# The channel-major copy of the activations: turned by transposing DMAs in DRAM instead of by TensorE

## The chip, the cores and the metric

The kernel runs on one core of one Trainium2 chip. The metric is the device time of one launch in microseconds (us). Work is spread over TensorE (PE, with its weight loads listed as PEld), VectorE (DVE), ScalarE (ACT), GpSimd (POOL) and the DMA engines; nearly all DMAs are issued by SyncE (SP), in program order, into one queue.

## The reference

Four residual blocks are applied one after the other to a sequence of 2048 tokens with 1024 channels, all in float32. Each block has the same frame and its own mixers:

```python
h = x @ w_in                       # 1024 -> the channels of the mixers
mixed = concat(mixers(h))          # recurrences, attention, gated parts
z = x + mixed @ w_out              # 1024 -> 1024
x = layer_norm(z) * ln_g + ln_b    # blocks 1 to 3
```

Block 1 has a chunked recurrence (HGRN2) and sliding-window attention; block 2 a gated linear attention (GLA, chunks with a running state) and a spatial gating part whose input is normalised; block 3 a retention and a multi-scale pool; block 4, which normalises its input by its root mean square first, has a band attention, an mLSTM and a convolution. Within a block a token needs only itself and earlier tokens.

## The kernel before

The sequence is cut into four blocks of 512 tokens, and a **stage** is one layer of one block. Stages run in pairs of blocks: layer 1 of blocks 0 and 1, layer 2 of blocks 0 and 1, up to layer 4, and then the same for blocks 2 and 3. In what follows (2,0) is layer 2 of block 0. There are 16 stages, and 12 of them (layers 1 to 3) leave an activation that a later stage reads.

A stage reads its activation **by channel**: channels lie on partitions, tokens along the row. `load_x` fetches it in eight pieces of 128x512 into `u` tiles and splits each into a high part `ah` (a ScalarE cast to the rounded fp32r type) and a low part `al` (VectorE, the difference). Every product with weights is then three matmuls: high by high, high by low, low by high. Weights come in pieces. In the first pass over a layer a raw piece is loaded into `wst` (two buffers), split into `whl`, and stored in DRAM as `wdr`; later passes load `whl` from `wdr` ready split, 1 MB a piece, into four `whl` buffers. `next_w` hands out the next piece. The in-projection is a row of matmuls named `acc<-whl,ah`, `acc<-ah,whl` and the like; the mixers' small matmuls and transposes write to `mm` (PSUM). Then `out_proj` multiplies by `w_out`, adds the residual rows and normalises them in `big`, by token.

The normalised rows must be turned round for the next layer. That is `tail`, once for each 128 tokens: eight PE transposes (`mm<-ident,big`), ScalarE copies out of PSUM into two `t` tiles, two DMAs to the channel-major DRAM buffer `chn`, and a DMA of the rows themselves to `rows` (the next layer's residual). For tiles with an odd number the normalisation is already complete; for even ones the layer's scale and bias are applied by ScalarE in the copy (by channel), and VectorE applies them to the rows. The four tails of a stage wait in `self.pending`; `flush`, called at later groups of the in-projection, takes one out in the **next** stage. So (1,0) is turned during (1,1), and read by `load_x` of (2,0) after it.

Program order is not the final order. A list scheduler fixes, before the run, the static order of instructions on each engine; weights have a high priority. Each engine then works through its list in order and waits on semaphores. Scratch tiles come from rings: the tag `t` has 7 buffers of 2 KB a partition, handed out in program order to tails, to the mixers' exponentials and states and to much else, so a later `t` tile can't be written before the tile seven requests earlier has been read for the last time. The PSUM tag `mm` has four banks, `acc` four.

Of the kernel before, what the change touches and what calls it, by code (L numbers as in the profile page):

```python
# [10 lines left out]
F32 = mybir.dt.float32  # L11
F32R = mybir.dt.float32r
I32 = mybir.dt.int32
U8 = mybir.dt.uint8
BF16 = mybir.dt.bfloat16
AF = mybir.ActivationFunctionType
ALU = mybir.AluOpType
# [3 lines left out]
D = 1024  # L21
T = 2048
TB = 512
# [203 lines left out]
class Build:  # L227
# [114 lines left out]
    def setup(self):  # L342
        nc = self.nc
# [14 lines left out]
        nc.gpsimd.affine_select(out=cm, in_=ones[:, 0:128], compare_op=ALU.is_ge, fill=0.0, base=0, pattern=[[1, 128]], channel_multiplier=-1)  # L358
        self.cmask = self.const([128, 128], U8, "cmask")
        nc.vector.tensor_copy(self.cmask, cm)  # L360
# [3 lines left out]
        nc.gpsimd.affine_select(out=self.amask, in_=zero, compare_op=ALU.is_ge, fill=NEGB, base=0, pattern=[[1, 128]], channel_multiplier=-1)  # L364
        self.rst = self.const([128, 512], BF16, "rst")
        nc.vector.memset(self.rst, 1.0)
# [7 lines left out]
        self.pending, self.ahead, self.start = [], [], True  # L374
        self.kv, self.kv_at, self.turn = None, None, 0

        self.chn, self.rows = {}, {}
        for l in self.layers[:-1]:
            for i in range(2):
                self.chn[l, i] = self.dp.tile([4, 128, D], F32, tag=f"chn{l}{i}", name="chn")  # L380
                self.rows[l, i] = self.dp.tile([4, 128, D], F32, tag=f"rows{l}{i}", name="rows")

        lb = self.const([128, 4], F32, "lb")
# [15 lines left out]
        for n in ("hgw", "glag", "retg", "pscale", "mlg"):  # L399
            h = self.const([128, 4], F32, n + "h")  # L400
# [93 lines left out]
    def next_w(self, n=1024):  # L494
        if self.ahead:
            return self.ahead.pop(0)
        w = self.weight(self.wi, self.wpos, n)
        self.wpos += 1
        return w

    def group(self, ps, w, a, b):
# [54 lines left out]

    def load_x(self, b, l):
        if not self.start:
            for t in range(4):
                for i in range(2):  # L560
                    self.load_x1(b, l, t, i)
            return

        ws = []
        self.wi, self.wpos = "wi1", 0
        for parts in (((0, 0), (1, 0)), ((0, 1), (1, 1)), ((2, 0), (3, 0)), ((2, 1), (3, 1))):
            for t, i in parts:
                with self.hp():
                    self.load_x1(b, l, t, i)
            ws.append(self.next_w())  # L570
        self.ahead, self.start = ws, False
        self.lc = self.lconst(l, b)
        with self.later(300):
            self.save()
# [5 lines left out]
    def load_x1(self, b, l, t, i):  # L580
        nc = self.nc
        st = self.u()
        src = self.I["xt"][b] if l == 1 else self.chn[l - 1, b % 2]
        self.first(nc.sync.dma_start(st, src[t, :, i * 512:i * 512 + 512]))
        c = slice(t * 128, t * 128 + 128)
        h = self.ah[:, 4 * i:4 * i + 4, c]
        nc.scalar.copy(h, c4(st))  # L587
        self.tt(self.al[:, 4 * i:4 * i + 4, c], c4(st), h.bitcast(F32), ALU.subtract)

    def load_xr(self, b, l):  # L590
        self.xr = self.big(self.at, [128, 4, D], F32)
# [22 lines left out]
    def out_proj(self, layer, b, split):  # L614
        nc = self.nc
        wo = f"wo{layer}"
        alpha = {1: ALPHA1, 2: ALPHA2, 3: ALPHA2, 4: 1.0}[layer]
        last = layer == max(self.layers)
        if layer < 4:
            lng, lnb = [self.u() for _ in range(2)], [self.u() for _ in range(2)]  # L620
            for i in range(2):
                nc.sync.dma_start(lng[i], self.I["lnp"][2 * layer - 2:2 * layer - 1, i * 512:i * 512 + 512].partition_broadcast(128))
                nc.sync.dma_start(lnb[i], self.I["lnp"][2 * layer - 1:2 * layer, i * 512:i * 512 + 512].partition_broadcast(128))
        acc = [self.acc() for _ in range(4)]
        for j in range(4):
            hi, lo = self.weight(wo, j)
            hi = hi.rearrange("p (k c) -> p k c", k=2)
            lo = lo.rearrange("p (k c) -> p k c", k=2)
            if j == 0:
                split(0)  # L630
                split(1)
            for i in range(2):
                for t in range(4):
                    self.out_mm(acc[t], t, 2 * j + i, hi[:, i], lo[:, i])
                    if j < 3 and i == 1 and t == 1:
                        split(2 * j + 2)
                        split(2 * j + 3)
        sts = []
        for t in range(4):
            x = self.xr[:, t, 0:512]  # L640
            self.stt(x, x, alpha, acc[t], ALU.mult, ALU.add)
            if layer < 4:
                st = self.s(12, "bst")
                nc.vector.bn_stats(st[:, 0:6], x)
                sts.append(st)
        if self.todo:
            self.lc = self.lconst(*self.todo[0])
        ws = []
        acc = [self.acc() for _ in range(4)]
        for j in range(4):  # L650
            hi, lo = self.weight(wo, 4 + j)
            ws.append((hi.rearrange("p (k c) -> p k c", k=2), lo.rearrange("p (k c) -> p k c", k=2)))
        for t in range(4):

            if t % 2 == 0:
                for k in range(8):
                    hi, lo = ws[k // 2]
                    for t1 in (t, t + 1):
                        self.out_mm(acc[t1], t1, k, hi[:, k % 2], lo[:, k % 2])
            x = self.xr[:, t, 512:1024]  # L660
            self.stt(x, x, alpha, acc[t], ALU.mult, ALU.add)
            if layer == 4:
                nc.sync.dma_start(self.O[b * TB + t * 128:b * TB + t * 128 + 128, :], self.xr[:, t])
                continue
            st = sts[t]
            nc.vector.bn_stats(st[:, 6:12], x)
            x = self.xr[:, t]
            mv = self.s(2, "mv")
            nc.vector.bn_aggr(mv, st)
            y = self.rstd1(mv[:, 1:2], 1.0, 1e-5)  # L670
            if not last and t % 2 == 0:
                nm = self.s(1, "nm")
                self.stt(nm, mv[:, 0:1], -1.0, y, ALU.mult, ALU.mult)
                self.act(x, x, AF.Identity, scale=y, bias=nm)
                continue
            for i in range(2):
                xi = x[:, i * 512:i * 512 + 512]
                self.stt(xi, xi, mv[:, 0:1], lng[i], ALU.subtract, ALU.mult)
                self.stt(xi, xi, y, lnb[i], ALU.mult, ALU.add)
            if last:  # L680
                nc.sync.dma_start(self.O[b * TB + t * 128:b * TB + t * 128 + 128, :], x)
        if not last:
            xr = self.xr
            self.pending = [lambda t=t: self.tail(layer, b, xr, t, lng, lnb) for t in range(4)]
            if layer == 3:
                self.pending.append(lambda: self.rms_row(b, xr))

    def tail(self, layer, b, xr, t, lng, lnb):

        nc = self.nc  # L690
        x = xr[:, t]
        for j in range(2):
            ps = self.mm()
            for i in range(4):
                k = 4 * j + i
                self.tr(ps[:, i * 128:i * 128 + 128], x[:, k * 128:k * 128 + 128])
            f = self.t()
            if t % 2 and layer < 3:
                nc.scalar.copy(f, ps)
            else:  # L700
                for i in range(4):
                    o = slice(i * 128, i * 128 + 128)
                    if t % 2:
                        self.act(f[:, o], ps[:, o], AF.Copy, scale=self.col("ng", 4 * j + i))
                    else:
                        k = 8 * (layer - 1) + 4 * j + i
                        self.act(f[:, o], ps[:, o], AF.Identity, scale=self.lgn[:, k:k + 1], bias=self.lbn[:, k:k + 1])
            nc.sync.dma_start(self.chn[layer, b % 2][t, :, j * 512:j * 512 + 512], f)
        if t % 2 == 0:
            for i in range(2):  # L710
                xi = x[:, i * 512:i * 512 + 512]
                self.tt(xi, xi, lng[i], ALU.mult)
                self.tt(xi, xi, lnb[i], ALU.add)
        nc.sync.dma_start(self.rows[layer, b % 2][t], x)

    def rms_row(self, b, xr):

# [1095 lines left out]
def c4(ap):  # L1813
    return ap.rearrange("p (a b) -> p a b", a=4)
# [22 lines left out]
```

## Time and profile before

| | |
|---|---|
| time, median of 3 runs | 3685.87 us (3685.3 to 3686.74) |
| time of the profiled execution | 3691.55 us |
| its span | 3689.8 us |
| PE idle in the span (span less busy) | 37.7 us |
| DVE / ACT busy | 2256.2 us (61%) / 1389.5 us (38%) |
| DMA moved | 798.03 MB |
| mean granted TensorE clock | 0.999 |

The span is the time from the first to the last instruction that the profiler saw; the profiled execution's own time is 1.75 us longer. A row of the profile's groups gives an operation (out<-in by tile name, shape, count), its busy time and the mean of one; a row of the timeline gives start, duration and what it waited for. An engine's instructions overlap in the pipeline, so on PE the pace is read from start to start.

### The profile page before, as it was taken

The page shows a single profiled execution, that of the slowest core. Times are in us where ns is not written, and L with a number is a line of the kernel's source. Part 1 is how long each engine was busy: PE and PEld are TensorE (multiplying, and loading weights), DVE is VectorE, ACT ScalarE, POOL GpSimd, SP SyncE. Part 2 cuts the span into 40 slices and gives each one's busy share as a digit, 9 for nine tenths or more (in the row PEclk, how much of TensorE's full clock was granted, in tenths as well). Part 3 has the DMA queues.
Part 4 walks back from the last instruction along what each step waited for, and adds up shares of the span by engine and source line. Part 5 has one row for each costly group of instructions (what it writes and reads, how often), then busy time and mean ns, then how long its engine had stood idle before and what let it go on. Part 6 is the DMA issues. An engine that isn't in the chain of part 4 may idle for free.

```text
span 3689.8 us, 53341 instructions
## 1 busy us (share of the span) xinstructions
PE 3652.1 (99%) x20576; PEld 3090.4 (84%) x20576; DVE 2256.2 (61%) x5796; ACT 1389.5 (38%) x2890; POOL 14.9 (0%) x37
## 2 busy tenths in 40 slices
PE   8999999999999999999999999999999999999999
PEld 7888888888787888888888888989887878888887
DVE  7765566555755598587556556444454546883874
ACT  6636343323341355235254372313121313541451
POOL 0000000000000000000000000000000000000000
PEclk9999999999999999999999999999999999999999
DMA  7784577856885784853644645657475747446534
GB/s 274 252 291 156 199 266 278 296 182 231 308 305 202 249 288 166 296 189 104 215 180 167 251 167 185 241 178 267 161 259 182 275 176 254 149 145 208 184 114 160
DMA packets 161823, 798.03 MB, mean 216 GB/s; under 512 B 17952, under 2 KB 18080, under 8 KB 93984
## 3 DMA queue, kind: packets, MB, share of 16 engines
q1 hardware_dynamic: 161568, 794.62, 60.6%
q8 instruction: 162, 2.65, 0.3%
q14 instruction: 93, 0.76, 0.1%
HBM read 593.02 MB, written 201.52 MB: 215 GB/s over the span
## 4 chain that ended last, share of the span: by engine, by line
PE 60%; DVE 3%; ACT 1%; issue 0%; DMA 0%; SPq 0%; POOL 0%; POOLq 0%; DVEq 0%; ACTq 0%
PE acc L324 50%; PE mm L324 7%; PE mm L327 3%; DVE u L312 1%; DVE t L315 0%; DVE whl L315 0%; DVE big L312 0%; ACT t L302 0%; ACT u L301 0%; ACT t L301 0%; DMA wst<-in_wi_dram 0%; ACT whl L458 0%; DVE ss L1437 0%; ACT big L301 0%; DMA chn<-t 0%
## 5 line engine op out<-in xcount | busy, mean ns | idle before, releaser
L324 PE MATMUL acc<-whl,ah 128*128 128x512 f32 (+3 forms) x6144 | 1815.2, 379 | 2.8 <-DVE mix L312 1.9
L324 PEld LDWEIGHTS acc<-whl,ah 128*128 128x128 f32 x6144 | 1111.7, 188 | 226.2 <-issue 4.8
L324 PE MATMUL acc<-whl,al 128*128 128x512 f32 (+3 forms) x3072 | 1159.0, 377 | 0.0
L324 PE MATMUL acc<-ah,whl 128*128 128x256 f32 (+1 forms) x4096 | 1062.4, 343 | 9.1 <-ACT whl L458 8.3
L324 PEld LDWEIGHTS acc<-ah,whl 128*128 128x128 f32 x4096 | 699.4, 189 | 92.2 <-ACT whl L458 8.5
L324 PE MATMUL acc<-al,whl 128*128 128x512 f32 (+1 forms) x2048 | 697.1, 340 | 0.0
L324 PEld LDWEIGHTS acc<-whl,al 128*128 128x128 f32 x3072 | 578.2, 188 | 114.4
L324 PEld LDWEIGHTS acc<-al,whl 128*128 128x128 f32 x2048 | 386.7, 189 | 40.0 <-issue 3.6
L315 DVE TENSOR_TENSOR whl<-wst,whl 128x1024 fp32r<-128x1024 f32 (+3 forms) x141 | 167.0, 1185 | 112.2 <-ACT whl L458 109.6
L458 ACT CAST whl<-wst 128x1024 fp32r<-128x1024 f32 (+3 forms) x141 | 143.4, 1019 | 169.2 <-PE acc L324 102.2
L587 ACT CAST ah<-u 128x512 fp32r<-128x512 f32 x128 | 78.4, 620 | 271.5 <-PE acc L324 249.2
L312 DVE SCALAR_TENSOR_TENSOR big<-big,acc 128x512 f32<-128x512 f32 x128 | 86.3, 680 | 134.9 <-PE acc L324 134.6
L312 DVE SCALAR_TENSOR_TENSOR u<-mix,hdw,u 128x512 f32<-128x512 f32 x240 | 166.2, 741 | 0.3
L312 DVE SCALAR_TENSOR_TENSOR g<-g,acc 128x512 f32<-128x512 f32 x80 | 55.0, 687 | 162.3 <-ACT g L301 162.0
L301 ACT ACTIVATE g<-acc 128x512 f32<-128x512 f32 x72 | 42.9, 597 | 236.6 <-PE acc L324 236.5
L315 DVE TENSOR_TENSOR al<-u,ah 128x512 fp32r<-128x512 f32 x128 | 86.7, 680 | 51.5 <-ACT ah L587 51.4
L301 ACT ACTIVATE t<-mm,cols 128x128 f32<-128x128 f32 (+2 forms) x272 | 98.3, 462 | 51.2 <-PE mm L327 48.5
L324 PE MATMUL mm<-big,u 128*128 128x256 f32 (+2 forms) x616 | 92.4, 285 | 1.3 <-DVE u L315 1.3
L324 PEld LDWEIGHTS mm<-big,u 128*128 128x128 f32 x616 | 83.8, 189 | 6.7 <-DVE u L315 1.5
L1020 DVE CUSTOM_DVE_ANT_0 t<-mm,lc,nsk 128x256 f32<-128x256 f32 (+1 forms) x128 | 55.0, 472 | 49.4 <-PE mm L324 49.1
L324 PEld LDWEIGHTS mm<-vb,t 128*128 128x128 f32 (+1 forms) x640 | 67.9, 169 | 16.1 <-issue 9.5
L324 PE MATMUL mm<-vb,t 128*64 128x128 f32 (+2 forms) x640 | 78.8, 278 | 1.6 <-DVE t L312 0.9
(338 smaller groups left out, 4062.3 us busy)
## 6 DMA issues: line engine op xcount, KB each, us to landing
whl<-wdr SPq DMA_DIRECT2D x396, 1024.0 KB, 4.8
wdr<-whl SPq DMA_DIRECT2D x132, 1024.0 KB, 4.9
wst<-in_wi_dram SPq DMA_DIRECT2D x99, 512.0 KB, 6.2
rows<-big SPq DMA_DIRECT2D x48, 512.0 KB, 4.7
chn<-t SPq DMA_DIRECT2D x96, 256.0 KB, 3.5
u<-chn SPq DMA_DIRECT2D x96, 256.0 KB, 7.0
big<-rows SPq DMA_DIRECT2D x48, 512.0 KB, 7.0
wst<-in_wo_dram SPq DMA_DIRECT2D x32, 512.0 KB, 5.7
```

Of the source, the lines that this page charges most:

```text
L301: return self.nc.scalar.activation(out, in_, f, bias=bias, scale=scale)
L312: return self.nc.vector.scalar_tensor_tensor(out, in0, s, in1, op0, op1)
L315: return (eng or self.nc.vector).tensor_tensor(out, a, b, op)
L324: return self.nc.tensor.matmul(out, lhsT, rhs, start=start, stop=stop)
L327: return self.nc.tensor.transpose(out, in_, self.ident)
L458: nc.scalar.copy(hi[:, c], st[:, c])
L587: nc.scalar.copy(h, c4(st))
L1020: nc.vector.tensor_tensor_reduce(out=p[:, o + off:o + 256], in0=ps[:, o + off:o + 256], in1=band[:, off:256], scale=-0.125, scalar=self.ns ...
```

## The change

Four things change. (1) `tail` no longer uses PE or PSUM. The rows are finished by VectorE first (even tiles get scale and bias before anything is read). Then each 32-bit value is taken apart: VectorE copies the low 16 bits of the row tile (128x1024) into a `t` tile, ScalarE the high 16 bits into another, and two DMAs write them to a new DRAM buffer `pln` (two planes of 512 tokens x 1024 channels). (2) After the fourth tail, eight closures are left in `self.turned`, one for each 128 channels. Each later call of `next_w`, once no tail is pending, runs one: two transposing DMAs (512x128 values of 16 bits each, 128 KB, to 128x512) into one `t` tile, a ScalarE copy and a VectorE copy which put the halves together in another `t` tile, and a DMA of 256 KB to `chn`. (3) `chn` is laid out by channel chunk, and `load_x2` reads two chunks by 256 tokens at a time, eight DMAs as before; layer 1 reads its input in sixteen DMAs of half the size. (4) The scale that layer 4 puts on its input moved from the tails of layer 3 into `load_x2`.

```diff
@@ next_w
         self.wpos += 1
+        if self.turned and not self.pending:
+            self.turned.pop(0)()
         return w
@@ load_x
-            for t in range(4):
-                for i in range(2):
-                    self.load_x1(b, l, t, i)
+            for c in range(0, TB, 256):
+                for k in range(0, 8, 2):
+                    self.load_x2(b, l, slice(c, c + 256), k)
+    def load_x2(self, b, l, c, k0):
+        nc = self.nc
+        st = self.u((128, 2, 256))
...
+            nc.sync.dma_start(st, self.chn[l - 1, b % 2][k0:k0 + 2, :, c].rearrange("k p t -> p k t"))
+        h, r = self.ah[:, k0:k0 + 2, c], self.al[:, k0:k0 + 2, c]
+        if l < 4:
+            nc.scalar.copy(h, st)
+            self.tt(r, st, h.bitcast(F32), ALU.subtract)
+            return
+        for k in range(2):
+            ng = self.col("ng", k0 + k)
+            self.act(h[:, k], st[:, k], AF.Copy, scale=ng)
+            self.stt(r[:, k], st[:, k], ng, h[:, k].bitcast(F32), ALU.mult, ALU.subtract)
@@ tail
-        for j in range(2):
-            ps = self.mm()
-            for i in range(4):
-                k = 4 * j + i
-                self.tr(ps[:, i * 128:i * 128 + 128], x[:, k * 128:k * 128 + 128])
-            f = self.t()
...
-            nc.sync.dma_start(self.chn[layer, b % 2][t, :, j * 512:j * 512 + 512], f)
         if t % 2 == 0:
             for i in range(2):
                 xi = x[:, i * 512:i * 512 + 512]
                 self.tt(xi, xi, lng[i], ALU.mult)
                 self.tt(xi, xi, lnb[i], ALU.add)
+        xv = x.bitcast(U16).rearrange("p (n w) -> p n w", w=2)
+        for w in range(2):
+            f = self.t((128, D), U16)
+            (nc.scalar.copy if w else nc.vector.tensor_copy)(f, xv[:, :, w])
+            nc.sync.dma_start(self.pln[layer, b % 2][w, t * 128:t * 128 + 128], f)
         nc.sync.dma_start(self.rows[layer, b % 2][t], x)
+        if t == 3:
+            self.turned = [lambda k=k: self.turn_planes(layer, b, k) for k in range(8)]
+    def turn_planes(self, layer, b, k):
+        nc = self.nc
+        pl, f = self.t((128, 2, TB), U16), self.t()
+        for w in range(2):
+            nc.sync.dma_start_transpose(pl[:, w], self.pln[layer, b % 2][w, :, k * 128:k * 128 + 128])
+        fv = f.bitcast(U16).rearrange("p (t w) -> p t w", w=2)
+        nc.scalar.copy(fv[:, :, 1], pl[:, 1])
+        nc.vector.tensor_copy(fv[:, :, 0], pl[:, 0])
+        nc.sync.dma_start(self.chn[layer, b % 2][k], f)
```

The new `t` tiles also move the lists of the scheduler. The first place is PE in stage (2,0), in the GLA of layer 2, whose chain runs from `mm<-t` (the decay logits, 128x512 x2) over `mm<-u` (scores), `mm<-vb,t` (the state's increment), `mm<-vb,am` and `mm<-t,u` (the outputs of a pair of chunks) to `mm<-u,lc` (spatial gating). Before, the rows of PE there read as follows, in the middle of the chain:

```order
L324 MATMUL mm<-vb,am_116 128x128 x4
L324 MATMUL mm<-vb,am_118 128x128 x4
L324 MATMUL mm<-t,u 128x128 x8
L324 MATMUL mm<-u 128x128 x8
L324 MATMUL acc<-whl,ah 128x512 x2
L324 MATMUL acc<-whl,al 128x512
L324 MATMUL acc<-whl,ah 128x512
L327 MATMUL mm<-ident,u 128x128 x4
```

After the change the same stage's PE list comes to the end of its in-projection (the first row here is its last matmul) and only then to the chain, from its first row on:

```order
L325 MATMUL acc<-whl,al 128x512
L325 MATMUL mm<-t 128x512 x2
L325 MATMUL mm<-u 128x128 x8
L328 MATMUL mm<-ident,u 128x128 x4
L325 MATMUL mm<-vb,t 64x128 x8
L325 MATMUL mm<-vb,am_116 128x128 x4
L325 MATMUL mm<-vb,am_118 128x128 x4
L325 MATMUL mm<-t,u 128x128 x2
L325 MATMUL mm<-u 128x128
L325 MATMUL mm<-t,u 128x128 x6
L325 MATMUL mm<-u 128x128 x7
L328 MATMUL mm<-ident,u 128x128 x4
```

What moved: the `acc` matmuls, which stood between the links of the chain, now all stand ahead of it, and no `acc` stands between two of its rows until the out-projection.

The second place is ACT in the same stage, at the chain's decays (`mix<-t`, `t<-t`). After the change, with `COPY t<-t` the high halves of turned chunks 4 to 7 and `COPY t<-mm` the copy of the transposed keys that the state's increment needs:

```order
L302 ACTIVATE mix<-t 128x512
L302 ACTIVATE t<-t 128x512
L302 ACTIVATE u<-acc 128x512
L741 COPY t<-t 128x512 x4
L836 COPY t<-mm 128x512
L303 ACTIVATE mix,ss<-mm 128x128 x8
```

Before, two weight casts and nothing of the tails stood between the decays and `COPY t<-mm`:

```order
L301 ACTIVATE mix<-t 128x512
L458 CAST whl<-wst 128x1024
L301 ACTIVATE t<-t 128x512
L458 CAST whl<-wst 128x1024
L807 COPY t<-mm 128x512
```

What moved: four copies, each of which waits for a pair of transposing DMAs, now stand ahead of `COPY t<-mm`.

The third place is SP, at the turns of stage (1,1). Before, the `chn` stores stood between loads of ready-split weights (`whl<-wdr`):

```order
L452 DMA whl<-wdr 128x2048
L708 DMA chn<-t 128x512
L452 DMA whl<-wdr 128x2048 x3
L708 DMA chn<-t 128x512
L452 DMA whl<-wdr 128x2048 x11
```

After the change a pair of transposing DMAs stands there for each chunk, and the store of a chunk, which waits for its pair and both copies, stands ahead of further weights:

```order
L456 DMA whl<-wdr 128x2048
L739 DMA_TRANSPOSE t<-pln 128x512 x2
L456 DMA whl<-wdr 128x2048
L743 DMA chn<-t 128x512
L739 DMA_TRANSPOSE t<-pln 128x512 x2
L743 DMA chn<-t 128x512
L739 DMA_TRANSPOSE t<-pln 128x512 x2
L456 DMA whl<-wdr 128x2048 x2
L743 DMA chn<-t 128x512
```

What moved: each chunk adds two issues and one wait to the queue that also carries the weights.

More of the change, by code (lines that the diff above doesn't have):

```diff
@@ L14 @@
 U8 = mybir.dt.uint8
+U16 = mybir.dt.uint16
 BF16 = mybir.dt.bfloat16
@@ L375, in setup @@
         self.kv, self.kv_at, self.turn = None, None, 0
-        self.chn, self.rows = {}, {}
+        self.chn, self.pln, self.rows = {}, {}, {}
+        self.turned = []
         for l in self.layers[:-1]:
             for i in range(2):
-                self.chn[l, i] = self.dp.tile([4, 128, D], F32, tag=f"chn{l}{i}", name="chn")
+                self.chn[l, i] = self.dp.tile([8, 128, TB], F32, tag=f"chn{l}{i}", name="chn")
+                self.pln[l, i] = self.dp.tile([2, TB, D], U16, tag=f"pln{l}{i}", name="pln")
                 self.rows[l, i] = self.dp.tile([4, 128, D], F32, tag=f"rows{l}{i}", name="rows")
@@ L582, in load_x1 @@
         st = self.u()
-        src = self.I["xt"][b] if l == 1 else self.chn[l - 1, b % 2]
-        self.first(nc.sync.dma_start(st, src[t, :, i * 512:i * 512 + 512]))
+        self.first(nc.sync.dma_start(st, self.I["xt"][b, t, :, i * 512:i * 512 + 512]))
         c = slice(t * 128, t * 128 + 128)
@@ L588, in load_x1 @@
         self.tt(self.al[:, 4 * i:4 * i + 4, c], c4(st), h.bitcast(F32), ALU.subtract)
+    def load_x2(self, b, l, c, k0):
+        nc = self.nc
+        st = self.u((128, 2, 256))
+        if l == 1:
+            for t in range(2):
+                t1 = c.start // 128 + t
+                nc.sync.dma_start(st[:, :, t * 128:t * 128 + 128], self.I["xt"][b, t1, :, k0 * 128:k0 * 128 + 256].rearrange("p (k t) -> p k t", k=2))
+        else:
+            nc.sync.dma_start(st, self.chn[l - 1, b % 2][k0:k0 + 2, :, c].rearrange("k p t -> p k t"))
[8 more added lines that the diff above has]
+            self.stt(r[:, k], st[:, k], ng, h[:, k].bitcast(F32), ALU.mult, ALU.subtract)
     def load_xr(self, b, l):
@@ L682, in out_proj @@
         if not last:
+            assert not self.turned
             xr = self.xr
@@ L691, in tail @@
         x = xr[:, t]
-        for j in range(2):
-            ps = self.mm()
-            for i in range(4):
-                k = 4 * j + i
-                self.tr(ps[:, i * 128:i * 128 + 128], x[:, k * 128:k * 128 + 128])
-            f = self.t()
[L698 to L707, printed above, removed]
-            nc.sync.dma_start(self.chn[layer, b % 2][t, :, j * 512:j * 512 + 512], f)
         if t % 2 == 0:
```

## The prediction

> **What bounds the kernel now.** I read the page's first two lines, then the windows by stage, then the waits of SP.
>
> ```profile
> span 3689.8 us, 53341 instructions
> PE 3652.1 (99%) x20576; PEld 3090.4 (84%) x20576; DVE 2256.2 (61%) x5796; ACT 1389.5 (38%) x2890; POOL 14.9 (0%) x37
> ...
> 450.00:690.00 240.00, 235.33 (x1332) 200.58 (x1331) 141.87 (x335) 89.21 (x160) 1.80 (x3) 0.99 0.79 278
> 690.00:862.00 172.00, 170.61 (x1048) 147.93 (x1047) 79.59 (x242) 51.92 (x115) 0.83 (x2) 1.00 0.61 217
> 1250.00:1380.00 130.00, 125.28 (x760) 110.24 (x759) 115.98 (x255) 77.87 (x142) 1.06 (x2) 0.99 0.84 292
> ...
> SPq L452 <- PE acc L324: 2078.9, 395, 13.6
> ```
>
> PE is idle for 3689.8 − 3652.1 = 37.7 us, so whatever leaves PE's list shortens the span, provided that nothing else comes late. The windows (length, busy of PE, PEld, DVE, ACT and POOL, granted clock, DMA share, GB/s) are stages (2,0) and (2,1) and the part with the densest VectorE work, (4,0). PE is full in each. SP waits 2078.9 us for PE to release a weight buffer (395 waits, 5.3 us each): the weights' queue runs ahead and has slack. PE stays full only because in-projection matmuls stand in its list between the links of the mixers' chains. That order is what the change can break.
>
> **Removed: the PE transposes.**
>
> ```profile
> L327 PE MATMUL mm<-ident,big 128*128 128x128 f32 x384 | 49.9, 273 | 1.7 <-ACT big L301 1.7
> ...
> 249.60 1.03 PE L327 MATMUL mm<-ident,big 128*128 128x128 f32 x8
> 250.39 0.37 PE L324 MATMUL acc<-ah,whl 128*128 128x256 f32 x1
> 250.59 0.28 PE L324 MATMUL acc<-al,whl 128*128 128x256 f32 x1
> ```
>
> 12 stages x 4 tails x 8 = 384 transposes, 48 groups of eight. From the start of a group to the next matmul is 0.79 us; that matmul's successor comes 0.20 us later instead of the usual 0.12, so the group holds PE 0.87 us. 48 x 0.87 = 41.8; bounds are 48 x 0.79 = 37.9 and the 49.9 busy. I take **−41 us**.
>
> **Added beside other work.**
>
> ```profile
> 250.23 2.91 ACT L301 ACTIVATE t<-mm,cols 128x128 f32<-128x128 f32 x8 [2.86 <-PE mm L327]
> ...
> L458 ACT CAST whl<-wst 128x1024 fp32r<-128x1024 f32 (+3 forms) x141 | 143.4, 1019 | 169.2 <-PE acc L324 102.2
> L315 DVE TENSOR_TENSOR whl<-wst,whl 128x1024 fp32r<-128x1024 f32 (+3 forms) x141 | 167.0, 1185 | 112.2 <-ACT whl L458 109.6
> L587 ACT CAST ah<-u 128x512 fp32r<-128x512 f32 x128 | 78.4, 620 | 271.5 <-PE acc L324 249.2
> L315 DVE TENSOR_TENSOR al<-u,ah 128x512 fp32r<-128x512 f32 x128 | 86.7, 680 | 51.5 <-ACT ah L587 51.4
> ```
>
> A stage adds to VectorE 4 copies of 128x1024 and 8 of 128x512. The trace shows no 16-bit copy; by the rows of equal element count it is 4 x 1.19 + 8 x 0.68 = 10.2 us, at the least nothing. ScalarE gets 4 x 1.02 + 8 x 0.62 = 9.0 us and loses the tails' copies (2.91 us for each of two tiles, and the plain ones): about even. In (2,1) VectorE has 92 us free and takes it. In (4,0) it has 14 free of 130, and I charge 4 us (bounds 0 and 10). The loads of the next stage keep number, element count and engines; layer 4's scale is only moved. DMA moves 2 MB into the planes and 2 MB back in each stage, 50 MB beside 798.03 (6%), under shares of 0.61 to 0.84: nothing by itself.
>
> **Added on SP: the turns.** The third excerpt of order shows the store of a chunk, which waits for its pair and the copies, ahead of the weights. No transposing DMA is in this trace. The nearest rows move 256 KB, as a pair does:
>
> ```profile
> whl<-wdr SPq DMA_DIRECT2D x396, 1024.0 KB, 4.8
> ...
> chn<-t SPq DMA_DIRECT2D x96, 256.0 KB, 3.5
> u<-chn SPq DMA_DIRECT2D x96, 256.0 KB, 7.0
> ...
> 452.64 0.63 PE L324 MATMUL acc<-whl,ah 128*128 128x512 f32 x2
> 453.11 0.40 PE L324 MATMUL acc<-whl,al 128*128 128x512 f32 x1
> 453.34 0.63 PE L324 MATMUL acc<-whl,ah 128*128 128x512 f32 x2
> ```
>
> Three matmuls take 0.70 us start to start, so a piece of 24 lasts PE 5.6 us. One turn holds the queue for the pair's landing x, the copies and their place in two other lists (1.8 us; the 0.68 copy is its floor) and issues (0.75, three by about a quarter; my choice). With about one piece of weights between turns it costs (x + 2.55 − 5.6) per chunk, eight times, less the cover: three loaded pieces, 3 x 5.6 − 4.8 landing = 12 to 13 us. It is free up to x = 13/8 + 3.05 = 4.7 us. By the `chn<-t` row (3.5) it costs nothing, by `u<-chn` (7.0) 8 x 3.95 − 13 = 18.6 us in each of nine stages that stream ready-split weights while they turn ((1,1), (1,3), (2,1), (2,2), (2,3), (3,1), (3,2), (3,3), (4,2)): 167 us. I take a landing under 4.7: `whl<-wdr` goes the same way, out of DRAM, and has four times the bytes in place after 4.8, while the 7.0 belongs to loads issued eight behind one another. The 7.0 is kept for the range.
>
> [...]
>
> **Moved: the order of PE.** This decides the sign. In (2,0), by the first excerpt, all in-projection pieces now come ahead of the GLA chain. Before, the chain ran under them:
>
> ```profile
> 525.04 0.17 DVE L1138 COPY lrt<-acc 128x16 f32<-128x16 f32 x1 [0.41 <-ACT vb L1137]
> ...
> 531.91 0.70 PE L324 MATMUL mm<-t 96*128 96x512 f32 x2 [2.82 <-DVE t L315]
> ...
> 547.72 0.69 DVE L312 SCALAR_TENSOR_TENSOR u<-u,t 128x512 f32<-128x512 f32 x1
> ...
> 561.14 0.69 DVE L315 TENSOR_TENSOR t<-mm,em 128x512 f32<-128x512 f32 x1 [3.83 <-PE mm L324]
> ...
> 564.50 0.29 DVE L1202 BATCH_NORM_STATS2 st<-u 128x6 f32<-128x128 f32 x1
> 564.70 0.55 DVE L315 TENSOR_TENSOR t<-t,em 128x384 f32<-128x384 f32 x1
> ...
> 588.49 1.42 DVE L315 TENSOR_TENSOR u<-u,lc 128x512 f32<-128x512 f32 x2
> ...
> 625.35 3.96 DVE L312 SCALAR_TENSOR_TENSOR mix<-mm,cols,u 128x128 f32<-128x128 f32 x15
> ```
>
> Step by step, with nothing for PE to do between:
> - (a) from the end of the run to `mm<-t`: 531.91 − 525.04 = 6.9 us before, with a weight split inside; 4 (bounds 2 and 6.9).
> - (b) from `mm<-t` to the last decay, 547.72 + 0.69 − 531.91 = 16.5 with three splits of 1.2 among them; 16 (bounds 13 and 16.5).
> - (c) to the state's first row `t<-mm,em`. Ahead of it on VectorE the new list has the whole normalisation of the gating input (564.50 to 589.91 before, 25.4 us with other work in it) and four copies of chunks; on ACT the four copies stand ahead of `COPY t<-mm`. The normalisation's own rows come to about 15 us, the copies to 4 x 0.68: 20 (bounds 10, if it is done by then, and 29, four turns of x + 2.55 with x = 4.7).
> - (d) two state chains (561.14 to 565.25, 4.1 us, each), two normalisations of outputs, the 16 gating rows (4.2 us by the last row) and the split for the out-projection: 21 (bounds 14 and 25).
>
> 61 us in all. PE's own rows inside (76 of 128x128 or 64x128, a pace of 0.1 us, 0.70 for `mm<-t` and about 1 us of gaps) are 10 us, so PE idles 51, less the 4.7 that this window had: **+46** (bounds 25 and 62).
>
> In (2,1), (2,2) and (2,3) the new list puts 10.5 us of `acc` between `mm<-t` and `mm<-u` where there were 20, and none round the state's rows:
>
> ```profile
> 737.25 0.70 PE L324 MATMUL mm<-t 96*128 96x512 f32 x2
> ...
> 749.70 0.68 DVE L312 SCALAR_TENSOR_TENSOR u<-u,t 128x512 f32<-128x512 f32 x1
> ...
> 766.50 0.69 DVE L315 TENSOR_TENSOR t<-mm,em 128x512 f32<-128x512 f32 x1 [5.87 <-PE mm L324]
> ...
> 768.84 0.56 DVE L315 TENSOR_TENSOR t<-t,em 128x384 f32<-128x384 f32 x1
> ...
> 772.07 1.95 PE L324 MATMUL mm<-vb,am 128*128 128x128 f32 x16
> ```
>
> The decays take 749.70 + 0.68 − 737.25 = 13.1: 13.1 − 0.5 − 10.5 = 2 us bare. The state's rows take 2.9, with 1 us of `mm<-vb,am` beside them: 2 bare, twice. 6 us a stage, **+18** (bounds 6 and 33). (3,0) and (3,1) lose some `acc` rows round the same kind of chain, 3 each; (1,1) and (1,3) have attention in another order, 4 each: **+14** (bounds 0 and 25). With (4,0) **+4**. These five stages are my estimates from the state's 2.9 us.
>
> **Sum.** 46 + 18 + 14 + 4 = 82 us of new idle, less 41 of transposes: +41. The profiled execution has 3691.55 us, 1.75 above its span; 3691.55 + 41 = 3732.6. It lies 5.7 above the median shown, so **3727 us**.
>
> **Rivals.**
> - *Slow transposing DMAs*: x is 7 us or more, and the weights come late behind the stores of chunks. For: the `u<-chn` row, the same size out of DRAM; the single in-order queue. Against: 2078.9 us of slack on it. 3727 + 167 = 3894, more for a larger x. [...]
> - *Faster, the chain stays short*: chunks 4 to 7 and the gating's normalisation are done before `mm<-t`, since their inputs come earlier in the projection, and the decays overlap the last pieces. (2,0) then idles 20 and the rest 8: 3691.55 − 41 + 28 − 5.7 = 3673. It decides when the new idle falls under 41 us. Against: the fixed lists put these rows behind the decays' rows.
> - *Even*: (2,0) at its lower bound, 25, the rest 16: 41 against 41, 3686.
>
> **Chances.** Forecast (3693 to 3770) 0.53, slow DMAs 0.27, faster 0.12, even 0.08. 0.2% is 7 us, about what a measurement of this kernel can tell from no change. Faster 0.12, same 0.08, slower 0.80. The range 3670 to 3900 leaves out half of the faster case and half of the slow one, 0.2.
>
> **What would show it.** Right: `mm<-ident,big` gone; (2,0) with some 50 us of idle PE, waiting for DVE and ACT rows in the chain, not for `whl`; pairs landing within 4.7 us; SP still waiting long for PE. Wrong: PE waits for `whl` in the stages that stream, the DMA_TRANSPOSE row over 5 us (slow DMAs); or (2,0) with 25 us idle or less.

## The result, and the profile after

The changed kernel takes 3812.78 us (median of 4 runs, 3808.9 to 3816.58) where the kernel before, run beside it, takes 3686.27: a ratio of 1.0343, 95% interval 1.0326 to 1.0361. It is slower, as forecast, but by 126.5 us and not by 41.

The first lines of the page, then the waits of PE (us in total, times, the longest) and of SP, after the change:

```profile
span 3810.6 us, 53232 instructions
PE 3649.8 (96%) x20192; PEld 3068.9 (81%) x20192; DVE 2338.0 (61%) x5972; ACT 1416.2 (37%) x2778; POOL 14.8 (0%) x37
...
PE acc L325 <- ACT t L302: 57.6, 2, 41.9
PE mm L325 <- ACT t L836: 37.2, 12, 20.0
PE mm L325 <- DVE u L313: 15.2, 2, 14.7
PE mm L325 <- DVE t L316: 10.4, 7, 3.2
PE acc L325 <- ACT whl L462: 7.8, 1, 7.8
...
SPq L456 <- PE acc L325: 1739.4, 363, 14.9
```

The 384 transposes are gone (20576 − 20192). Yet PE is busy almost as long as before (3652.1), and idle for 160.8 us instead of 37.7. Nearly all of the new idle stands in a handful of waits for ACT and DVE; the one wait for weights (7.8) is that of the start, and SP still waits 1739 us for PE. Two waits make up the first row: 41.9 us, and 15.7.

Where they lie is shown by the windows of the four stages that grew most, (2,0), (3,0), (4,0) and (4,2), cut at the last residual addition of each stage (length, PE busy, granted clock, DMA share, GB/s); before the change first, then after:

```profile
489.10:697.40 208.30, 203.63 (x1183) 0.99 0.83 294
904.70:1081.70 177.00, 175.72 (x945) 1.00 0.87 308
1262.40:1550.80 288.40, 281.27 (x1551) 0.99 0.75 262
3088.20:3387.70 299.50, 299.15 (x1708) 1.00 0.52 182
```

```profile
485.90:732.40 246.50, 206.60 (x1171) 0.91 0.81 269
939.30:1131.60 192.30, 180.38 (x928) 0.96 0.89 298
1311.90:1637.40 325.50, 282.65 (x1552) 0.93 0.70 246
3192.80:3507.90 315.10, 298.24 (x1678) 0.97 0.55 187
```

They grew by 38.2, 15.3, 37.1 and 15.6 us, 106 of the 120.8 by which the span grew. The clock column shows a second loss: matmuls that are left run at a lower granted clock there (0.91, 0.96, 0.93 and 0.97; before 0.99, 1.00, 0.99 and 1.00).

The longest wait is in (4,0). ACT's timeline (start, duration, operation, what it waited for), the first and the last of the copies of eight turns and the rows round them:

```profile
1376.41 1.04 ACT L462 CAST whl<-wst 128x1024 fp32r<-128x1024 f32 x1 [4.12 <-DMA wst<-in_wi_dram]
1390.33 0.76 ACT L741 COPY t<-t 128x512 uint16<-128x512 uint16 x1 [12.88 <-DMA t<-pln]
1392.86 0.76 ACT L741 COPY t<-t 128x512 uint16<-128x512 uint16 x1 [1.76 <-DMA t<-pln]
...
1411.68 0.76 ACT L741 COPY t<-t 128x512 uint16<-128x512 uint16 x1 [2.46 <-DMA t<-pln]
1412.31 1.07 ACT L302 ACTIVATE t<-acc 128x512 f32<-128x512 f32 x2
```

and SP's over the same time:

```profile
1379.84 0.32 SPq L483 DMA_DIRECT2D wdr<-whl  x1
1380.21 0.42 SPq L477 DMA_DIRECT2D wst<-in_wi_dram  x1
1380.68 0.92 SPq L729 DMA_DIRECT2D pln<-t  x1
1381.65 1.46 SPq L730 DMA_DIRECT2D rows<-big  x1
1383.16 8.27 SPq L739 DMA_TRANSPOSE t<-pln  x4
1391.54 0.51 SPq L743 DMA_DIRECT2D chn<-t  x1
1392.10 2.46 SPq L739 DMA_TRANSPOSE t<-pln  x2
```

The reader is to see a chain. The last write of a plane stands in SP's list behind raw weights: ScalarE had copied its half by 1330.1 and VectorE, in the row below, by 1330.2, and SP issues the write at 1380.68.

```profile
1329.52 0.68 DVE L728 COPY t<-big 128x1024 uint16<-128x1024 uint16 x1
```

So the turns begin at 1383; each then takes 3.1 us (1392.10 to 1395.23, from pair to pair); and `t<-acc`, which empties the PSUM banks that PE needs for its next matmul, comes after all eight. PE stands still from 1371.1 to 1412.9.

### The profile page after: what moved, and what is told of

It is laid out like the page before. It is cut to its first block, busy times and chain, and to the rows that moved or that the text cites. A ratio compares the mean times of both kernels' runs of the same rounds, so it can differ in the third digit from the quotient of the medians.

```text
span 3810.6 us, 53232 instructions
## 1 busy us (share of the span) xinstructions
PE 3649.8 (96%) x20192; PEld 3068.9 (81%) x20192; DVE 2338.0 (61%) x5972; ACT 1416.2 (37%) x2778; POOL 14.8 (0%) x37
## 5 line engine op out<-in xcount | busy, mean ns | idle before, releaser
L325 PE MATMUL acc<-ah,whl 128*128 128x256 f32 (+1 forms) x4096 | 1048.7, 342 | 7.8 <-ACT whl L462 7.8
L325 PEld LDWEIGHTS acc<-al,whl 128*128 128x128 f32 x2048 | 387.8, 189 | 41.9 <-issue 3.1
L741 ACT COPY t<-t 128x512 uint16<-128x512 uint16 x96 | 74.0, 771 | 332.8 <-DMA t<-pln 233.9
L742 DVE COPY t<-t 128x512 uint16<-128x512 uint16 x96 | 44.0, 458 | 230.3 <-DMA t<-pln 226.3
L608 ACT CAST ah<-u 128x512 fp32r<-128x512 f32 x88 | 54.2, 620 | 205.0 <-PE acc L325 193.2
L325 PE MATMUL mm<-vb,t 128*64 128x128 f32 (+2 forms) x640 | 82.6, 293 | 37.2 <-ACT t L836 37.2
L316 DVE TENSOR_TENSOR al<-u,ah 128x512 fp32r<-128x512 f32 x96 | 64.5, 679 | 52.1 <-ACT ah L608 50.7
```

Of the source, the lines that this page charges most:

```text
L316: return (eng or self.nc.vector).tensor_tensor(out, a, b, op)
L325: return self.nc.tensor.matmul(out, lhsT, rhs, start=start, stop=stop)
L608: nc.scalar.copy(h, st)
L741: nc.scalar.copy(fv[:, :, 1], pl[:, 1])
L742: nc.vector.tensor_copy(fv[:, :, 0], pl[:, 0])
```

## The experiments

Theory A: turns take their tiles from the ring `t`. Each of eight turns takes two of its slots, one until both copies have read it and one until a store far back in SP's list, and the mixers' tiles, `t<-acc` among them, come behind them. That makes the lists of PE and ACT what they are, and the waits. Rival B: the transposing DMAs themselves, by their time on the queue. Rival C: the copies of a turn, which wait for DMAs in the lists of ACT and DVE, ahead of what PE needs.

**A ring of their own.**

```diff
-        pl, f = self.t((128, 2, TB), U16), self.t()
+        pl = self.tp.tile([128, 2, TB], U16, tag="pl", name="t", bufs=2)
+        f = self.tp.tile([128, 512], F32, tag="pl", name="t", bufs=2)
```

> The two tiles of a turn come from a ring of their own (two buffers of 2 KB) instead of the seven of tag t; everything else is the change. Theory A (the turns hold slots of the ring t, and by that the fixed lists and the waits of PE are what they are): PE's list in (2,0) is that of before again, the 41.9 us wait in (4,0) and the 35 us in (2,0) go, PE idle falls from 161 us to 30 to 60, time 3640 to 3690. Rival B (the transposing DMAs hold the queue: 192 issues of 1.23 us): they are all still there, time 3780 or more. Rival C (the copies of a turn stand in the lists of ACT and DVE and wait for DMAs there): the copies are still there, idle stays over 100 us, time over 3740.

Measured: 3697.91 us, ratio to before 1.0033 (1.0022 to 1.0045). 115 of the 126 us are gone, with every transposing DMA and every copy still there, by two buffers. PE's list in (2,0) has 20.3 us of `acc` between `mm<-t` and `mm<-u` again and 5.7 on each side of `mm<-vb,t`; in (4,0) `t<-acc` stands behind casts of weights and no copy. Its span, PE busy and first waits:

```profile
span 3694.6 us, 53229 instructions
PE 3627.3 (98%) x20192; PEld 3058.0 (83%) x20192; DVE 2324.8 (63%) x5972; ACT 1415.1 (38%) x2778; POOL 15.0 (0%) x37
...
PE mm L328 <- DVE nq L316: 11.8, 6, 6.7
PE acc L325 <- ACT ah L608: 11.1, 1, 11.1
```

67 us idle, against an expected 30 to 60, and the time 8 us above the expected 3640 to 3690. Theory A holds in the main, with something left over; B and C, which had it over 3740, fall as the main cause.

**The copies on GpSimd, in the shared ring.**

```diff
-        nc.scalar.copy(fv[:, :, 1], pl[:, 1])
-        nc.vector.tensor_copy(fv[:, :, 0], pl[:, 0])
+        nc.gpsimd.tensor_copy(fv[:, :, 1], pl[:, 1])
+        nc.gpsimd.tensor_copy(fv[:, :, 0], pl[:, 0])
```

> Both copies of a turn run on GpSimd; the tiles stay in the ring t. Theory A (slots of the ring): later t tiles still wait for the turns' slots; (4,0) keeps most of its 41.9 us and (2,0) most of its 40, time 3780 to 3830, more if GpSimd's copies are slow. Rival C (the copies stand in ACT's list ahead of what PE needs): the waits for ACT of 41.9, 20.0 and 15.7 us go, time about 3812 - 80 = 3730. Rival B: as the change, 3800 to 3825.

Measured: 3797.94 us, ratio 1.0299 (1.0284 to 1.0315). No copy stands in ACT's list now, and the wait in (4,0) is still 39.6 us. ACT's row there names it:

```profile
1392.43 1.08 ACT L302 ACTIVATE t<-acc 128x512 f32<-128x512 f32 x2 [32.14 <-POOL t L741]
```

`t<-acc` has its input since PE stopped. It waits for GpSimd's copies, that is for the slot which its output is to get. That it is the slot is read from the names of the two rows; the profile names the releaser and not the reason. Moving the copies only changed whom it waits for. Rival C had a part in the chains of layers 2 and 3: in (2,0) the 20.0 us for `ACT t L836` became 6.8, since the key copy no longer stands behind four copies, and over the whole kernel the 37.2 us of this row became 7.5; in (4,2) the wait grew from 15.7 to 31.2. The time alone would fit rival B nearly as well (3800 to 3825); it is the ring of their own that speaks against B.

**Both edits.**

> Both: a ring of their own, copies on GpSimd. Theory A: within 0.5% of the run with the ring alone, 3640 to 3690. Rival C: faster than the ring alone by 1% or more. Rival B: 3780 or more.

Measured: 3678.39 us, ratio 0.9975 (0.9964 to 0.9985): faster than before by a quarter of a per cent, and 0.5% faster than the ring alone. Neither form of the expectation is met exactly; once the ring is out of the way, moving the copies is worth 19.5 us. How much of that is the copies' own time, and how much the static lists, which move with them, no run separates.

**Plain DMAs of the same size**, in the shared ring:

```diff
-            nc.sync.dma_start_transpose(pl[:, w], self.pln[layer, b % 2][w, :, k * 128:k * 128 + 128])
+            nc.sync.dma_start(pl[:, w], self.pln[layer, b % 2][w, 64 * k:64 * k + 64].rearrange("t (a c) -> (t a) c", a=2))
```

> Each transposing DMA is replaced by a plain DMA of the same 128 KB from the same planes into the same tile; nothing is turned, so this leaves the transposition out. PE's list in (2,0) and ACT's eight copies in (4,0) stay. Theory A: a turn's loop on the queue falls from 3.1 us by the shorter issues (0.4 for 1.23, twice) to about 1.8, so the waits in (4,0), (2,0) and (4,2) shrink by some 10 us each, time 3770 to 3795. Rival B: nearly all goes, 3650 to 3700. Rival C: as theory A.

Measured: 3778.83 us, ratio 1.0249 (1.0234 to 1.0265), as theory A had it. The waits in (4,0) and (2,0) remain, 35.5 and 18.7 + 14.8 us: with a DMA that turns nothing 92 of the 126 us stay, and 34 go.

**Nine buffers in the shared ring.**

```diff
-        self.tp = pool("tp", 7)
+        self.tp = pool("tp", 9)
```

> The change with nine buffers in the ring t instead of seven, the memory of the run with a ring of its own, but turns and mixers still take turns in one ring. Theory A in the form 'what counts is that a turn's slots stand between the mixers' in one ring': the list of PE in (2,0) is that of the change, time 3780 to 3815. Theory A in the form 'there are too few buffers': 3680 to 3720, as with the ring of its own.

Measured: 3820.02 us, ratio 1.036 (1.0346 to 1.0374), 5 us above the range of the first form and 100 above that of the second. The same memory as the ring of its own, and nothing gained: it isn't the number of buffers but that 16 requests of the turns stand between those of the mixers.

**The kernel before with nine buffers**, as a control:

> The kernel before with nine buffers of t, a control for the memory: nothing waits there for t (PE idle 37.7 us, most of it at the start), so 3680 to 3690, no difference that can be told.

Measured: 3690.74 us, ratio 1.001 (1.0001 to 1.0019): the memory alone gives nothing (0.1% the other way).

**The transposing DMAs twice, and not at all, with the ring of their own.**

```diff
+            nc.sync.dma_start_transpose(pl[:, w], self.pln[layer, b % 2][w, :, k * 128:k * 128 + 128])
```

> The ring of its own with ACT and DVE copies, and every transposing DMA issued twice (192 more, the second writes the same). Theory A (the transfers are hidden once they hold no mixer's slot): 3700 to 3735. Rival B (192 issues of 1.23 us on the queue show): +236 us, 3900 and more.

Measured: 3789.3 us, ratio 1.0278 (1.0263 to 1.0292), 91 us over the ring alone: between the two. 192 more issues are some 236 us of SP's time (192 x 1.23, an estimate from the row of a pair, 2.46, after the change), and the kernel's time grew by two fifths of that.

> The ring of its own with ACT and DVE copies, and each transposing DMA replaced by a plain DMA of the same 128 KB (nothing is turned: the transposition is left out). Doubling the transposing DMAs in this ring cost 91 us, so they are not free: if a transposing DMA's longer issue (1.23 us for some 0.4) is what shows, this falls under the run with the ring alone, 3698, by some 20 to 45 us, 3653 to 3678. If the doubling only overran a slack that one set of them leaves whole, it stays at 3690 to 3700, and what is left is the copies' and stores' doing.

Measured: 3680.15 us, ratio 0.9981 (0.9972 to 0.9991), 18 us under the ring alone, just under the expected gain. Rival B is real at about this size, 18 us in the ring of its own and 34 in the shared one, not 126. The static lists of the two runs are not quite the same (213 of 20192 matmuls and 118 of 2715 rows of ScalarE stand at another place), so not all of the 18 need be time on the queue.

**What is left of waits.** The longest single one with a ring of its own is `ACT ah L608`, 11.1 to 12.4 us. It ends at 1086.5 us in the run with the ring alone, where (3,1) begins: it is the load of (3,1), which needs the last turn of (2,1), and that turn runs at the end of (3,0). The expectations that follow call it the load of (4,0) behind turns in (3,1), one stage too late. Four buffers in the ring (`bufs=4`, copies on GpSimd):

> The ring of its own with four buffers, copies on GpSimd. The 12.4 us that the load of (4,0) waits with two buffers, for the last turns in (3,1), go if two turns can be in flight: 3655 to 3672. If the last turns are late for their place in SP's list instead: 3672 to 3685, no change.

Measured: 3678.03 us, ratio 0.9978 (0.9968 to 0.9987); the wait is 12.3 us as ever, as the second form had it. Three edits on top of it try the turns' place in the list: two turns per `next_w`, all eight at one, and one at the weights' priority.

> As the run with four buffers and GpSimd copies, and each next_w takes out two turns instead of one. If the 12.3 us that the load of (4,0) waits come from the last turn's place in SP's list (one row ahead of the loads of chn in (3,1), eleven rows with this edit): they go with their slow clock, 3660 to 3670. If the turns' transfers themselves are late: 3675 to 3685, as before the edit.

> All eight turns are taken out at one next_w. By the place in the list: as with two per piece, 3660 to 3670. By the queue's slack (eight pairs of transposing DMAs between fewer weights): 3670 to 3690.

> One turn per next_w, at the weights' priority, so that turns no longer stand behind weights in SP's list. If late turns are what is left: 3655 to 3670. If the weights then come late behind the turns (a turn holds the queue some 3 us of 5.6): 3690 or more, with PE waiting for whl.

Measured: 3685.24 (ratio 0.9993, 0.9984 to 1.0003), 3684.66 (0.9996, 0.9987 to 1.0005) and 3687.09 us (1.0002, 0.9992 to 1.0012). None is faster. The first lies just above its second range, the second within its second one. The third lies between its two: PE waits for `whl<-wdr` now, but only 3.8 us. With two per piece the wait in front of (3,1) does go, as the first form said, and the time does not fall: one of 11.8 us comes up in (3,0), in front of PE's `acc`, where the residual addition waits 8.7 us for the load of its rows:

```profile
PE mm L328 <- DVE nq L316: 12.0, 7, 3.2
PE acc L325 <- DVE big L313: 11.8, 1, 11.8
```

Each placement makes another list. The best version found is the ring of its own with GpSimd's copies, with two buffers or four, 0.2 to 0.25% under the kernel before.

## Why the prediction was right in sign and wrong in size

*What was right.* The fixed lists decide, the kernel gets slower, and the weights do not run short. But the time lies in none of the four cases with a chance: the forecast ended at 3770, and slow DMAs had 3894. In (2,0) the chain stands bare, as the order of PE's rows said, and its steps can be read off PE's timeline:

```profile
623.10 0.70 PE L325 MATMUL mm<-t 96*128 96x512 f32 x2 [1.67 <-DVE t L316]
638.54 2.08 PE L325 MATMUL mm<-u 64*128 64x128 f32 x16 [14.74 <-DVE u L313]
640.55 1.11 PE L328 MATMUL mm<-ident,u 128*128 128x128 f32 x4
661.66 1.98 PE L325 MATMUL mm<-vb,t 128*64 128x128 f32 x16 [20.00 <-ACT t L836]
```

By PE's waits step (a) was 1.7 us for 4, (b) 14.7 for 16, (c) 20.0 for 20. That (c) agrees is in part luck: with the copies on GpSimd the same wait is 6.8 us, so some 13 of the 20 belong to the place of the copies in the lists, where the prediction had 15 for a normalisation and 2.7 for copies. Step (d), the states and the outputs, was to take 21; after 661.7 no wait is over 1.6 us, as two pairs of chunks fill each other's gaps. The stage got 35 us of new idle instead of 46.

*The transposes*: stages that got no new wait show their worth. (3,3), before, and with the ring of its own:

```profile
2910.80:3088.20 177.40, 177.23 (x962) 1.00 0.62 225
```

```profile
2917.00:3090.50 173.50, 173.33 (x927) 1.00 0.77 254
```

3.9 us, and 3.4 in (2,2) (205.3 to 201.9), for the 41 / 12 = 3.4 of the prediction.

*The step that failed* is the term of (4,0): "In (4,0) it has 14 free of 130, and I charge 4 us (bounds 0 and 10)." It asked whether VectorE has time for its copies, and not what stands in the lists behind tiles that wait; the prediction looks at no list of (4,0), and has no term for a slot of `t`. ACT's list there has eight `COPY t<-t` directly ahead of `t<-acc`. What was counted was time; what ran out was slots, and (4,0) got 35.7 us of new idle. (4,2), which was counted among the stages that stream weights and got no term for its lists, has the same rows and got 16.5; (3,0), set at 3, got 10.6. The whole, in new idle: predicted 46 + 18 + 14 + 4 = 82, measured 123 (160.8 − 37.7). By terms: 46 for (2,0) became 35; 18 for (2,1), (2,2) and (2,3) became 10; 14 for (3,0), (3,1), (1,1) and (1,3) became 18; 4 for (4,0) became 36; the 17 of (4,2) and 7 in the other stages had no term. The windows that the prediction calls (2,1) and (4,0) are not the whole stages, either: these were 698 to 905 and 1263 to 1551 us, so the 14 of 130 is the first part of (4,0).

*A term that was not in the sum* is the clock. PE's rows after the wait in (4,0), then its windows (length, busy, clock, DMA share, GB/s):

```profile
1412.95 0.80 PE L325 MATMUL acc<-whl,ah 128*128 128x256 f32 x2 [41.88 <-ACT t L302]
...
1413.76 0.63 PE L325 MATMUL acc<-whl,ah 128*128 128x256 f32 x2
...
1414.39 0.63 PE L325 MATMUL acc<-whl,ah 128*128 128x256 f32 x2
...
1419.31 0.40 PE L325 MATMUL acc<-whl,ah 128*128 128x256 f32 x2
...
1419.67 0.39 PE L325 MATMUL acc<-whl,ah 128*128 128x256 f32 x2
```

```profile
1405.00:1410.00 5.00, 0.00 (x0) 0.50 0.64 184
1410.00:1415.00 5.00, 2.05 (x9) 0.50 0.42 136
1415.00:1420.00 5.00, 5.00 (x29) 0.59 0.00 0
1420.00:1425.00 5.00, 5.00 (x45) 1.00 0.06 26
```

Three matmuls take 0.63 us from start to start, and 0.36 once the clock is back, 6.3 us after the restart: some 2.7 us (6.3 x (1 − 0.36 / 0.63)) lost on top of the wait. Summed over windows of 2 us (busy time by the share of the clock that is missing) it is 27.1 us after the change and 3.2 before; at the pace of the rows above, 0.57 of the full one, the difference would be some 21 and not 24. The account then reads 123 + 24 − 41 = 106 of 120.8. The other 15 lie in PE's busy time, most of them in the small matmuls of the chains of layers 2 and 3. Two of their rows, before, then after:

```profile
L324 PE MATMUL mm<-t,u 64*128 64x128 f32 x256 | 18.6, 285 | 0.0
L324 PE MATMUL mm<-u 64*128 64x128 f32 x256 | 17.8, 278 | 0.0
```

```profile
L325 PE MATMUL mm<-t,u 64*128 64x128 f32 x256 | 25.5, 315 | 9.1 <-DVE t L1286 7.8 <-DVE t L313 0.8 <-DVE t L316 0.5
L325 PE MATMUL mm<-u 64*128 64x128 f32 x256 | 25.2, 291 | 15.2 <-DVE u L313 15.2
```

With `mm<-vb,t` (128*64) and `mm<-vb,am` these rows have 109.7 us before and 132.5 after. In the run with a ring of their own, where `acc` stands round them as before, the same account leaves 2 us and not 15: 29.6 of new idle (67.3 − 37.7), 14 of slow clock (17.2, summed in the same way, less 3.2) and −41 are 3 of the 4.8 by which its span grew. Of the 22.8 about 10 lie at half clock and are counted above; some 13 are left. That they stand alone is a likely reason; no run shows it by itself.

*The rival of slow transposing DMAs* had the wrong mechanism, and so had the term in the sum that was set at nothing. A transposing DMA of 128 KB lands 4.5 us after its issue (median of 192); the plain one of the same size lands after 4.5 in the shared ring and 4.7 in the ring of its own:

```profile
t<-pln SPq DMA_TRANSPOSE x192, 4.5
```

The x of the prediction is the landing of a pair, and the second DMA is issued some 1.2 us after the first: 5.7 us, the median of the 96 pairs in the trace. That is over the 4.7 that were to be free, so this sign of being right was not met; by the prediction's sum it would cost 8 x (5.7 + 2.55 − 5.6) − 13 = 8 us in each of nine stages, by late weights. The quarter for an issue in its 2.55 was its author's choice: before, SP took 0.32 for a `chn<-t` and 0.45 for a `u<-chn` (medians). But weights did not come late, since turns overlap (four transposing DMAs stand ahead of the first store in SP's rows above) and SP still waits 1739 us for PE. What costs is the issue, 2.46 us for a pair (above), and the runs with plain DMAs put 18 to 34 us on it where the sum had nothing. In plain form, in the run with a ring of their own, SP's row for a pair reads:

```profile
301.26 0.89 SPq L740 DMA_DIRECT2D t<-pln  x2
```

## What to carry to other kernels

In this kernel tiles taken from a shared ring held up what asked next, whichever engine worked on them: PE's wait in (4,0) was 41.9 us with the copies on ScalarE and VectorE and 39.6 with them on GpSimd. Where a tile waits for a far-off DMA, try a ring of its own: two buffers did there (3697.91 us) what two more in the shared ring did not (3820.02). In the lists of the changed program look at ACT and DVE as well as at PE: ask, for each row that PE waits for, which row stands ahead of it and which slot its output gets. Count a stall of PE by its length and by the slow clock behind it (here 41.9 us, and some 2.7 behind it).

## What the runs showed of the hardware

A transposing DMA of 128 KB held SP's queue for 1.23 us (2.46 a pair, in (4,0) for pair after pair; four pairs in (3,0) of the run with the ring alone took 2.7 to 3.2; the median of all 192 after the change is 1.25), a plain one of the same size 0.45 (0.89 a pair; of the five pairs from 290 to 345 us of that run four took 0.86 to 0.92 and one 1.77). In the wait of 41.9 us, from 1371.1 on, the granted clock was 1.00 until 1374, 0.67 in the next 2 us and 0.50 from 1376; PE then worked at 0.50 for 6.3 us (three matmuls in 0.63). After the wait of 15.7 us in (4,2) three matmuls took 0.64 us from start to start for 4.6 us, and 0.36 after that. The 16-bit copies took 0.46 us on VectorE and 0.77 on ScalarE, where rows of the same number of 32-bit elements (`al<-u,ah`, a difference on VectorE; `ah<-u`, a cast on ScalarE) took 0.68 and 0.62:

```profile
L741 ACT COPY t<-t 128x512 uint16<-128x512 uint16 x96 | 74.0, 771 | 332.8 <-DMA t<-pln 233.9
L742 DVE COPY t<-t 128x512 uint16<-128x512 uint16 x96 | 44.0, 458 | 230.3 <-DMA t<-pln 226.3
```
